# Expert pairs in one block of TensorE, a gather of four experts in two float32r parts, seventeen weight slots

## The chip, the cores and the metric

One core of a Trainium2 chip runs the whole program. The metric is device time in microseconds (us) of one execution. The engines named here: PE (TensorE, matrix products; PEld is its load of stationary operands, which lies beside the products), DVE (VectorE), ACT (ScalarE), POOL (GpSimd) and SP (SyncE), whose queue issues all the DMAs of this kernel in one order.

## The reference, cut to what matters

Two blocks follow each other for 256 tokens of 1024 numbers: a hybrid block (three kinds of token mixing, then a mixture of experts) and a block of feed-forward layers, gating and attention. All is float32. The change lies in the mixture of experts:

```
for gi in range(N_GROUPS):                      # 4 groups of 8 experts
    hg = silu(einsum('nd,edf->nef', x, wg[gi])) * einsum('nd,edf->nef', x, wu[gi])
    y = y + einsum('nef,efd->nd', hg * gates[:, gi, :, None], wd[gi])
```

Each token has two experts of the 32; `gates` is zero for the others. An expert has two matrices of 1024 x 512 and one of 512 x 1024, 6 MB of float32, so the 32 of them are 192 loads of 1 MB.

## The kernel before

Ahead of the experts a mixing stage runs to about 620 us, with its weights split into two float32r parts each (`mm3`, lines 276 to 278: three products for one). After the experts come four feed-forward layers of the same kind, the first through `ffn(0)`.

The expert stage computes only the tokens that an expert has. `route` finds for each expert the rank of every token in its list; `places(p)` makes a one-hot matrix `oh` of 256 tokens by 64 places for each of the two experts of pair p on DVE, and `gather(p)` multiplies the normed tokens `xn` (named `xnr` in the rows) by it on PE, in float32: 16 products of a 128 x 128 stationary operand with 128 columns, in the trace 32 rows. ACT adds shift and gain and writes `xg`. There are 16 pairs, and a gather stands one pair ahead.

`pair` does the rest. `both` takes two weight slots, one for each expert, and issues for every k two products of 64 stationary columns with 512 columns of weights: expert 0 into rows 0 to 63 of a PSUM tile, expert 1 into rows 64 to 127. Where the two stand next to each other on PE they run side by side, in different columns of the array. A pair has four calls of `both` for the gate and up matrices and two for the down matrix, 48 such products, 96 rows (line 1211; a float32 product has two rows). Between them lie four transposes of the activated product (line 1232), two of `oh` (1239), two small products for the gates (1241), and `spread`, eight float32r products (lines 1262, 1263) that bring the pair's result back to the tokens.

In each pair a list `order` fixes the order of the products of `both` among themselves; where the gather's products and those of `spread` stand between them is left to the scheduler of the framework. After every `both`, `load_slot` puts two loads on SP's queue, into the slots just read. There are 19 slots of 1 MB: `wp`, `wr` (half of what held the hi and lo parts of the activations in the mixing stage; the other half holds `xn`), eight `we`, four `wx`, three `ws` and two `whl`, the last two kinds shared with the weight staging of the layers before and after. A load waits until PE has read the slot's old content, and a matrix product until its load has landed. Each load counts on one of eight semaphores in turn, so that a load also waits for the eighth load before it.

After pair 0, `overflow` reads the longest list and branches on all engines around code for lists over 64, which is not run with these inputs (line 1407). PSUM holds a ring of four `mm` tiles for all of this, and four `bg` tiles for `spread`.

Of the kernel before, what the change touches and what calls it, by code (L numbers as in the profile page):

```python
# [8 lines left out]
F32 = mybir.dt.float32  # L9
F32R = mybir.dt.float32r  # L10
# [9 lines left out]
S = 256  # L20
# [13 lines left out]
WS, WHL, WH2 = 3, 3, 3  # L34
NE_B8, NE_MIX, NSLOT = 8, 4, 19
ADA_EVERY, ADA_FROM = 3, 6
# [145 lines left out]
class Program:  # L182
# [280 lines left out]
    def run(self):  # L463
        tc, nc, d = self.tc, self.nc, self.d
        with ExitStack() as es:
# [36 lines left out]
            eights.close()  # L502
            self.parts()
            self.whx = es.enter_context(tc.tile_pool(name="whx", bufs=1))
# [16 lines left out]
            self.last_norm(g)  # L521

    def parts(self):
        self.hi, self.lo = [self.main.tile([128, KT, S], F32R, name=n, tag="hl", bufs=2) for n in ("hi", "lo")]

# [614 lines left out]
    def experts(self):  # L1140


        nc, tc, d, V = self.nc, self.tc, self.d, self.nc.vector
        km, C, exs = self.km, self.cap_limit, self.exs
        iota = km[:, 192:320]
        self.xn, spare = [self.main.tile([128, 2, 1024], F32, name=n, tag="hl", bufs=2) for n in ("xnr", "wr")]
        with tc.tile_pool(name="exw", bufs=1) as self.exw:
            self.slots.append(spare.rearrange("p a c -> p (a c)"))
            self.slots += [self.b8([128, 2048], name="we") for _ in range(NE_B8)]
            xgs = self.b8([128, 2, KT, 2, CAP], name="xg")  # L1150
# [8 lines left out]
            def places(p):  # L1159

                e2 = slice(2 * p, 2 * p + 2)
                ohs[p] = oh = exs.tile([128, 2, 2, CAP], F32, name="oh", bufs=2)
                V.tensor_tensor(oh, iota[:, None, None, :CAP].to_broadcast([128, 2, 2, CAP]),
                                rank[:, :, e2, None].to_broadcast([128, 2, 2, CAP]), op=OP.is_equal)
                if C < CAP:
                    V.memset(oh[..., C:], 0.0)

            def gather(p):

                oh, xg = ohs[p], xgs[:, p % 2]  # L1170
                for k0 in range(0, KT, 4):
                    ps = self.mms().rearrange("p (k a c) -> p k a c", k=4, a=2)
                    for k in range(k0, k0 + 4):
                        for t in range(2):
                            nc.tensor.matmul(ps[:, k - k0], self.xn[:, t, k * 128:k * 128 + 128], oh[:, t], start=(t == 0), stop=(t == 1))  # L1175
                        gain, shift = self.a2c[:, k:k + 1], self.sh2c[:, k:k + 1]
                        nc.scalar.activation(xg[:, k], ps[:, k - k0], AF.Identity, bias=shift, scale=gain)

            places(0)
            gate, rgs = gates()  # L1180
            gather(0)
            pend = None
            for p in range(NE // 2):

                def ahead():
                    if p + 1 < NE // 2:
                        places(p + 1)
                        gather(p + 1)

                pend = self.pair(p, xgs[:, p % 2], ohs[p], gate, yp, pend, ahead)  # L1190
# [11 lines left out]

    def both(self, outs, xs, ks, w, order):


        ws = [self.slots[(self.nuse + j) % NSLOT] for j in range(2)]
        self.nuse += 2
        for k in ks:
            for ps, c in outs:
                for j in range(2):  # L1210
                    ins = self.nc.tensor.matmul(ps[j * 64:j * 64 + 64], xs(k)[j], w(ws[j], k, c), start=(k == 0), stop=(k == order[1]))  # L1211
                    self.chain(order[0], ins)
        for _ in range(2):
            self.load_slot()

    def pair(self, p, xg, oh, gate, yp, pend, ahead):
        nc, exs, V = self.nc, self.exs, self.nc.vector
        e0, order = 2 * p, []
        ps = []
        for z in range(2):  # L1220
            ps.append(self.mms())
            for u in range(2):
                self.both([(ps[z], 0)], lambda k: [xg[:, k, j] for j in range(2)], range(4 * u, 4 * u + 4),
                          lambda w, k, c: w[:, k % 4 * 512:k % 4 * 512 + 512], (order, KT - 1))
        a = exs.tile([128, 512], F32, name="act")
# [5 lines left out]
        for ft in range(4):  # L1231
            nc.tensor.transpose(pt[:, ft * 128:ft * 128 + 128], a[:, ft * 128:ft * 128 + 128], self.ident)  # L1232
        at = exs.tile([128, 4, 2, CAP], F32, name="actT")
        nc.scalar.copy(at.rearrange("p a b c -> p (a b c)"), pt)

        po = self.mms()
        o2 = [oh[:, t].rearrange("p a c -> p (a c)") for t in range(2)]
        for t in range(2):
            nc.tensor.transpose(po[:, t * 128:t * 128 + 128], o2[t], self.ident)
        for t in range(2):  # L1240
            nc.tensor.matmul(po[:, 256:258], o2[t], gate[:, t, e0:e0 + 2], start=(t == 0), stop=(t == 1))
        ot = self.exw.tile([128, S], F32R, name="ot", bufs=2)
# [6 lines left out]
        for h in range(2):  # L1249
            pd = self.mms()  # L1250
            self.both([(pd, 0)], lambda k: [at[:, k, j] for j in range(2)], range(4),
                      lambda w, k, c: w[:, k * 512:k * 512 + 512], (order, 3))
            nc.scalar.activation(dh[:, h], pd, AF.Copy, scale=gs)
            V.scalar_tensor_tensor(dl[:, h], pd, gs, dh[:, h].bitcast(F32), op0=OP.mult, op1=OP.subtract)
        return p, dh, dl, ot, yp

    def spread(self, p, dh, dl, ot, yp):

        for h in range(2):
            for t in range(2):  # L1260
                o = ot[:, t * 128:t * 128 + 128]
                self.nc.tensor.matmul(yp[t][h], o, dl[:, h], start=(p == 0), stop=False)  # L1262
                self.nc.tensor.matmul(yp[t][h], o, dh[:, h], start=False, stop=(p == NE // 2 - 1))  # L1263

    def route(self, km):
# [7 lines left out]
        def sm(n, name):  # L1273
            return small.tile([128, 2, n], F32, name=name)
# [10 lines left out]
        xT = self.whl([128, 2, KT, 128], F32, True)  # L1285
        ss, rs, lg = sm(2, "ssr"), small.tile([128, 2], F32, name="rsr"), sm(36, "lg")
        for h in range(2):
            self.res(0, h)
# [37 lines left out]
        logits(0)  # L1326
        self.chain(edge[1], nc.scalar.activation(self.xn[:, 0], self.x[:, 0], AF.Copy, scale=rs[:, 0:1]))
        evac(1, 0)
# [4 lines left out]
        self.chain(edge[1], nc.scalar.activation(junk[:, :1], self.ones[:, :1], AF.Exp))  # L1333
        self.chain(edge[1], nc.scalar.activation(self.xn[:, 1], self.x[:, 1], AF.Copy, scale=rs[:, 1:2]))
        self.res = self.rest = self.edge = None
# [21 lines left out]
        sel = small.tile([128, 2, NE], F32R, name="sel")  # L1357
        V.tensor_mul(sel.rearrange("p a (g e) -> p a g e", g=4), og4, ssel[:, :, None, :].to_broadcast([128, 2, 4, 8]))
        pk = self.mms()[:, :2 * NE].rearrange("p (a b) -> p a b", a=2)
# [37 lines left out]
    def overflow(self, topi, rgs, iota):  # L1397
# [9 lines left out]
        with tc.If(n > C):  # L1407
            nc.sync.dma_start(rg.rearrange("e p c -> p e c"), rgs)
            with tc.For_i(0, NE) as e:
                with tc.tile_pool(name="ov", bufs=1) as ov:  # L1410
# [8 lines left out]
                    for c0 in range(C, S, 128):  # L1419
# [15 lines left out]
                        for k in range(KT):  # L1435
                            ps = mm()[:, :128]
                            for t in range(2):
                                nc.tensor.matmul(ps, self.xn[:, t, k * 128:k * 128 + 128], oh[:, t], start=(t == 0), stop=(t == 1))
# [4 lines left out]
                        s, at = [exs.tile([128, 512], F32, name=n) for n in ("act", "actT")]  # L1443
                        nc.scalar.activation(s, pz[0], AF.Silu)
# [383 lines left out]
```

## Time and profile before

| | |
|---|---|
| median of 3 runs | 2152.36 us (2151.04 to 2152.95) |
| profiled execution | 2148.5 us, span 2146.7 us |
| PE busy | 2083.3 us, 97% of the span |
| DVE, ACT busy | 1110.4 us (52%), 866.2 us (40%) |
| DMA | 503.20 MB, mean 234 GB/s |
| expert stage, first gather to last `spread` | 636.9 to 1141.8 us |

PE is busy nearly throughout. The slices of the page show that the DMA engines are half idle before and after the expert stage, at some 200 GB/s, and move about 410 GB/s within it. In the views below a window gives, for each engine, busy time and count of instructions, then the granted clock of PE (1.00 is 2.4 GHz, 0.50 is 1.2 GHz), the busy share of the DMA engines and their rate.

### The profile page before, as it was taken

The numbers are of one execution on the slowest core, as the hardware profiler recorded it, in microseconds if no ns is written. First come the engines' busy times: TensorE is split into PE (matmuls) and PEld (weight loads), VectorE is DVE, ScalarE is ACT, GpSimd is POOL, SyncE is SP. The second block draws the span as 40 slices with busy tenths as digits, with TensorE's granted clock in tenths as the row PEclk, the third lists the DMA queues.
The fourth block names the chain that finished last, engine by engine and source line by source line (L and its number), as shares of the span: only waits on it lengthen the run. The fifth ranks groups of instructions, "written<-read, shape, count | busy, mean of one in ns | idle before, by whom it ended". The sixth has DMA issues, their size and how long they took to land.

```text
span 2146.7 us, 29952 instructions
## 1 busy us (share of the span) xinstructions
PE 2083.3 (97%) x12484; PEld 1634.6 (76%) x12484; DVE 1110.4 (52%) x1602; ACT 866.2 (40%) x1264; POOL 24.7 (1%) x40
## 2 busy tenths in 40 slices
PE   7999999999988999999999999999999999999998
PEld 5889889877873444444447998878999999989997
DVE  5987867756450010001006555756555655686555
ACT  4444234344441222122115444645444544475443
POOL 0000000000000000000000000000000000000000
PEclk9999999999999999999999999999999999999999
DMA  8655445565677999999955555544555555533552
GB/s 331 239 192 206 177 174 182 195 233 196 217 303 321 409 416 411 410 396 411 404 209 206 180 193 197 209 174 145 209 182 191 178 180 194 177 118 138 190 183 98
DMA packets 72126, 503.20 MB, mean 234 GB/s; under 512 B 8218, under 2 KB 10034, under 8 KB 11698
## 3 DMA queue, kind: packets, MB, share of 16 engines
q1 hardware_dynamic: 71986, 501.24, 62.0%
q8 instruction: 99, 1.62, 0.3%
q14 instruction: 41, 0.34, 0.0%
HBM read 500.14 MB, written 1.07 MB: 233 GB/s over the span
## 4 chain that ended last, share of the span: by engine, by line
PE 65%; DVE 2%; ACT 1%; issue 0%; DMA 0%; POOLq 0%; DVEq 0%; POOL 0%; ACTq 0%
PE mm L1211 16%; PE mm L276 10%; PE mm L278 10%; PE mm L277 10%; PE bg L276 5%; PE bg L277 5%; PE bg L278 5%; PE mm L1175 3%; PE bg L1262 1%; PE bg L1263 1%; PE mm L419 1%; DVE act L1227 0%; PE mm L1232 0%; PE mm L1780 0%; PE mm L1743 0%
## 5 line engine op out<-in xcount | busy, mean ns | idle before, releaser
L256 DVE TENSOR_TENSOR whl<-ws,whl 128x1024 fp32r<-128x1024 f32 x228 | 277.7, 1220 | 220.9 <-ACT whl L255 220.1
L255 ACT CAST whl<-ws 128x1024 fp32r<-128x1024 f32 x228 | 238.4, 1048 | 295.3 <-PE mm L278 250.1
L256 DVE TENSOR_TENSOR wlx<-ws,whx 128x1024 fp32r<-128x1024 f32 x165 | 201.0, 1222 | 141.2 <-ACT whx L255 140.7
L255 ACT CAST whx<-ws 128x1024 fp32r<-128x1024 f32 x165 | 172.3, 1049 | 175.6 <-PE mm L278 100.3
L276 PE MATMUL mm<-hi,whl 128*128 128x256 f32 x836 | 235.4, 282 | 1.1 <-DVE whl L256 1.0
L277 PE MATMUL mm<-lo,whl 128*128 128x256 f32 x836 | 233.8, 280 | 0.1
L278 PE MATMUL mm<-hi,whl 128*128 128x256 f32 x836 | 233.3, 279 | 0.0
L256 DVE TENSOR_TENSOR whd<-ws,whd 128x1024 fp32r<-128x1024 f32 x113 | 137.7, 1219 | 112.0 <-ACT whd L255 111.2
L255 ACT CAST whd<-ws 128x1024 fp32r<-128x1024 f32 x113 | 118.2, 1046 | 172.7 <-PE mm L278 127.6
L276 PE MATMUL mm<-hi,wlx 128*128 128x256 f32 x640 | 179.4, 280 | 0.5 <-ACT rrow L1545 0.5
L277 PE MATMUL mm<-lo,whx 128*128 128x256 f32 x640 | 179.3, 280 | 0.0
L278 PE MATMUL mm<-hi,whx 128*128 128x256 f32 x640 | 179.2, 280 | 0.0
L276 PEld LDWEIGHTS mm<-hi,whl 128*128 128x128 f32 x836 | 157.2, 188 | 3.3 <-issue 1.2
L277 PEld LDWEIGHTS mm<-lo,whl 128*128 128x128 f32 x836 | 157.2, 188 | 1.5 <-DVE lo L620 0.7
L278 PEld LDWEIGHTS mm<-hi,whl 128*128 128x128 f32 x836 | 157.2, 188 | 0.2
L1227 DVE TENSOR_TENSOR act<-act,mm 128x512 f32<-128x512 f32 x16 | 11.0, 688 | 273.5 <-PE mm L1211 273.5
L276 PEld LDWEIGHTS mm<-hi,wlx 128*128 128x128 f32 x640 | 121.0, 189 | 1.9 <-ACT rrow L1545 0.8
L277 PEld LDWEIGHTS mm<-lo,whx 128*128 128x128 f32 x640 | 121.0, 189 | 0.7
L278 PEld LDWEIGHTS mm<-hi,whx 128*128 128x128 f32 x640 | 121.1, 189 | 0.0
L277 PE MATMUL mm<-whl,hi 128*128 128x512 f32 (+1 forms) x304 | 118.0, 388 | 0.0
L278 PE MATMUL mm<-whl,hi 128*128 128x512 f32 (+1 forms) x304 | 116.3, 383 | 0.0
L276 PE MATMUL mm<-whl,lo 128*128 128x512 f32 (+1 forms) x304 | 114.8, 391 | 1.2 <-DVE lo L433 1.2
(554 smaller groups left out, 4331.5 us busy)
## 6 DMA issues: line engine op xcount, KB each, us to landing
ws<-in_w_fi SPq DMA_DIRECT2D x88, 1024.0 KB, 4.8
we<-in_w_e SPq DMA_DIRECT2D x80, 1024.0 KB, 8.8
ws<-in_w_fo SPq DMA_DIRECT2D x44, 1024.0 KB, 4.7
ws<-in_w_a SPq DMA_DIRECT2D x40, 1024.0 KB, 4.7
wx<-in_w_e SPq DMA_DIRECT2D x40, 1024.0 KB, 8.6
ws<-in_w_e SPq DMA_DIRECT2D x30, 1024.0 KB, 8.8
ws<-in_w_b SPq DMA_DIRECT2D x26, 1024.0 KB, 4.9
whl<-in_w_e SPq DMA_DIRECT2D x20, 1024.0 KB, 6.9
```

The lines of the kernel that those rows point to most:

```text
L255: w1 = nc.scalar.copy(wh[:, :m], src)
L256: w2 = nc.vector.tensor_sub(wl[:, :m], src, wh[:, :m].bitcast(F32))
L276: first = mm(out, ll, rh, start=start, stop=False)
L277: mm(out, lh, rl, start=False, stop=False)
L278: self.last_mm = mm(out, lh, rh, start=False, stop=stop)
L419: ins = nc.tensor.transpose(pss[k % 2][:, (k // 2) * 128:(k // 2) * 128 + 128], self.x[:, t, k * 128:k * 128 + 128], self.ident)
L1175: nc.tensor.matmul(ps[:, k - k0], self.xn[:, t, k * 128:k * 128 + 128], oh[:, t], start=(t == 0), stop=(t == 1))
L1211: ins = self.nc.tensor.matmul(ps[j * 64:j * 64 + 64], xs(k)[j], w(ws[j], k, c), start=(k == 0), stop=(k == order[1]))
L1227: V.tensor_mul(a, a, ps[1])
L1262: self.nc.tensor.matmul(yp[t][h], o, dl[:, h], start=(p == 0), stop=False)
L1263: self.nc.tensor.matmul(yp[t][h], o, dh[:, h], start=False, stop=(p == NE // 2 - 1))
```

## The change

- The gather takes four experts at a time and float32r. `hi` and `lo` are now two tiles of their own for the whole program. In `route` they hold the normed tokens as `hh` (ACT, which wrote `xn` before) and the remainder `hl` (DVE, two new operations of 128 x 1024). A gather of four experts is, for each of the eight k, four products with 256 columns: the remainder and the main part for each half of the tokens. Half of it (four k, 16 products) is issued in each pair, for the four experts after the current ones; pair 0 also does the second half of the first four between its first and second `both`.
- One list `pe` fixes the whole order of PE in the stage: gather, `both`, transposes, `spread`. The products of `both` of a pair are not broken into any more.
- The `spread` of pair 0 is issued ahead of the branch.
- `wr` and one `we` are gone: 17 slots. `xg` takes two tiles instead of one, and `actT` moves to another pool.

The core of the diff:

```diff
-NE_B8, NE_MIX, NSLOT = 8, 4, 19
+NE_B8, NE_MIX, NSLOT = 7, 4, 17
...
-            self.parts()
+            self.hi, self.lo = [main.tile([128, KT, S], F32R, name=n) for n in ("hi", "lo")]
...
+                e4 = slice(4 * q, 4 * q + 4)
+                ohs[q] = oh = exs.tile([128, 2, 4, CAP], F32R, name="oh", bufs=2)
...
+            def gather(q, ks):
+                oh, xg = ohs[q], xgs[q % 2]
+                parts = [(hz, t) for t in range(2) for hz in (self.hl, self.hh)]
+                for k in ks:
+                    if k % 2 == 0:
+                        both = self.mms().rearrange("p (k a c) -> p k a c", k=2, a=4)
+                    ps = both[:, k % 2]
+                    for i, (hz, t) in enumerate(parts):
+                        self.chain(self.pe, nc.tensor.matmul(ps, hz[:, t, k * 128:k * 128 + 128], oh[:, t], start=(i == 0), stop=(i == 3)))
...
+                    if 4 * q < NE:
+                        if p % 2 == 0:
+                            places(q)
+                        gather(q, ks)
...
                 if p == 0:
+                    self.spread(*pend)
+                    pend, self.pe = None, []
                     self.overflow(topi, rgs, iota)
...
+                if p == 0 and z == 0 and u == 0:
+                    gather(0, range(4, KT))
...
+        self.chain(edge[0], V.scalar_tensor_tensor(hl[:, 0], self.x[:, 0], rs[:, 0:1], hh[:, 0].bitcast(F32), op0=OP.mult, op1=OP.subtract))
...
+        self.no_sync(V.scalar_tensor_tensor(hl[:, 1], self.x[:, 1], rs[:, 1:2], hh[:, 1].bitcast(F32), op0=OP.mult, op1=OP.subtract), found)
```

How PE's order changes in a pair well inside the stage. First before: from the transposes of one pair to the first piece of `spread` of the pair before (`k` is the identity, `we`, `wx`, `ws` weight slots, `whd` the result that `spread` brings back; x13 is thirteen in a row).

```order
L1239 MATMUL mm<-k_75,oh 128x128 x2
L1241 MATMUL mm<-gate,oh 128x2 x2
L1175 MATMUL mm<-oh,xnr 128x128 x4
L1211 MATMUL mm<-we,actT 64x512 x13
L1175 MATMUL mm<-oh,xnr 128x128 x4
L1211 MATMUL mm<-we,actT 64x512 x3
L1211 MATMUL mm<-wx,xg 64x512 x2
L1262 MATMUL bg<-whd,ot 128x512
```

The gather of the next pair (L1175) cuts the run of 16 down products after the thirteenth, between the two experts of one k, and `spread` cuts the next pair's gate products. Now after, from the last gate and up products of a pair to the start of its share of the gather:

```order
L1211 MATMUL mm<-ws,xg 64x512 x9
L1264 MATMUL bg<-whd,ot 128x512 x8
L1235 MATMUL mm<-k_75,act 128x128 x4
L1242 MATMUL mm<-k_75,oh 128x128 x2
L1244 MATMUL mm<-gate,oh 128x2 x2
L1172 MATMUL mm<-oh,lo 128x256
L1172 MATMUL mm<-oh,hi 128x256
```

`spread` has moved in one piece between the products and the transposes, which wait for DVE; behind the two last rows the gather goes on to its sixteen products in one piece, and then the 16 down products follow whole.

SP's queue at the start of the stage, before: the reloads behind pair 0 and the branch (`topi` is the longest list).

```order
L1401 TENSOR_LOAD topi
L1401 ISA x2
L1199 DMA wp<-in_w_e 128x2048
L1199 DMA wr<-in_w_e 128x2048
L1199 DMA we<-in_w_e 128x2048 x8
L1199 DMA wx<-in_w_e 128x2048 x2
L1407 COMPARE_AND_BRANCH
```

After:

```order
L1407 TENSOR_LOAD topi
L1407 ISA x2
L1200 DMA wp<-in_w_e 128x2048
L1200 DMA we<-in_w_e 128x2048 x7
L1200 DMA wx<-in_w_e 128x2048 x4
L1413 COMPARE_AND_BRANCH
```

Twelve reloads stand ahead of the branch on either side; those behind it go round 17 slots instead of 19.

On DVE, in `route` after the change, the second new operation stands between the choice of experts and the ranks:

```order
L1361 TENSOR_TENSOR ssel<-rp,ig 128x16
L1363 TENSOR_TENSOR sel<-og,ssel 128x64
L1364 SCALAR_TENSOR_TENSOR lo<-x,rsr,hi 128x1024
L1388 TENSOR_TENSOR wsel<-wsel,ssel 128x16
L1372 TENSOR_SCALAR rank<-sel 128x64
```

Before, the rows follow one another without the third; `rank` is what `oh` and with it the first gather wait for.

## Rows read from the trace of the kernel before

**Rows 1.** The waits of SP's queue, 600 to 1140 us (us, times, longest).

```profile
SPq L1199 <- PE mm L1211: 372.6, 126, 8.6
```

**Rows 2.** Windows of the expert stage (engines, PE clock, DMA share, GB/s).

```profile
650.00:675.00 25.00, 22.34 (x116) 10.89 (x112) 2.92 (x6) 7.63 (x14) 0.00 (x0) 1.00 1.01 423
656.00:660.00 4.00, 3.11 (x23) 2.06 (x20) 1.30 (x4) 0.83 (x2) 0.00 (x0) 1.00 1.02 430
685.00:690.00 5.00, 5.00 (x27) 1.71 (x23) 0.00 (x0) 0.60 (x1) 0.00 (x0) 1.00 0.72 257
737.00:768.00 31.00, 30.11 (x150) 13.35 (x148) 2.93 (x6) 6.55 (x14) 0.00 (x0) 1.00 1.01 413
```

**Rows 3.** PE from pair to pair, timeline (start, us, line, out<-in, xcount, idle before).

```profile
849.80 0.49 PE L1232 MATMUL mm<-k,act 128*128 128x128 f32 x3
...
850.71 1.14 PE L1175 MATMUL mm<-oh,xnr 128*128 128x128 f32 x8
851.78 4.51 PE L1211 MATMUL mm<-we,actT 128*64 128x512 f32 x18
...
861.23 0.40 PE L1263 MATMUL bg<-whd,ot 128*128 128x512 f32 x1
861.46 0.39 PE L1262 MATMUL bg<-whd,ot 128*128 128x512 f32 x1
...
880.25 0.66 PE L1232 MATMUL mm<-k,act 128*128 128x128 f32 x4 [0.89 <-DVE act L1227]
...
883.31 0.59 PE L1211 MATMUL mm<-ws,actT 128*64 128x512 f32 x1
...
883.74 0.59 PE L1211 MATMUL mm<-ws,actT 128*64 128x512 f32 x1
```

**Rows 4.** PE timeline: float32r products with 256 columns, at 1.2 and 2.4 GHz.

```profile
1148.35 0.41 PE L277 MATMUL mm<-whl,hi 128*128 128x256 f32 x1
1148.57 0.41 PE L278 MATMUL mm<-whl,hi 128*128 128x256 f32 x1
...
1161.39 0.28 PE L277 MATMUL mm<-lo,whx 128*128 128x256 f32 x1
1161.51 0.28 PE L278 MATMUL mm<-hi,whx 128*128 128x256 f32 x1
```

**Rows 5.** ACT's and DVE's groups by line that price the new operations.

```profile
L256 DVE TENSOR_TENSOR wlx<-ws,whx 128x1024 fp32r<-128x1024 f32 x165 | 201.0, 1222 | 141.2 <-ACT whx L255 140.7
L1177 ACT ACTIVATE xg<-mm,ada,a2c 128x128 f32<-128x128 f32 x126 | 55.3, 458 | 61.6 <-PE mm L1175 61.6
```

**Rows 6.** PE timeline around the start of the stage and the branch.

```profile
636.94 2.97 PE L1175 MATMUL mm<-oh,xnr 128*128 128x128 f32 x12 [0.44 <-DVE oh L1163]
...
646.73 10.47 PE L1211 MATMUL mm<-we,xg 128*64 128x512 f32 x48
...
672.18 1.05 PE L1175 MATMUL mm<-oh,xnr 128*128 128x128 f32 x8
679.14 6.31 PE L1211 MATMUL mm<-wx,xg 128*64 128x512 f32 x16 [5.91 <-PEq L1407]
685.27 4.03 PE L1211 MATMUL mm<-ws,xg 128*64 128x512 f32 x17
```

**Rows 7.** SP and PE timelines at the end of the stage.

```profile
1093.98 0.33 SPq L1199 DMA_DIRECT2D wr<-in_w_e  x1
...
1135.38 0.59 PE L1211 MATMUL mm<-wp,actT 128*64 128x512 f32 x1
...
1141.42 0.39 PE L1263 MATMUL bg<-whd,ot 128*128 128x512 f32 x1
```

**Rows 8.** DMA time from issue to landing: expert loads, then early ones (`adaf`).

```profile
DMA to landing us min/median/max: 4.7/8.7/13.6
...
DMA to landing us min/median/max: 13.6/16.0/20.4
```

**Rows 9.** Window of the early loads.

```profile
20.00:40.00 20.00, 20.00 (x114) 11.88 (x113) 13.92 (x40) 8.13 (x20) 0.49 (x2) 1.00 1.02 415
```

More of the change, by code (lines that the diff above doesn't have):

```diff
@@ L502, in run @@
             eights.close()
-            self.parts()
             self.whx = es.enter_context(tc.tile_pool(name="whx", bufs=1))
@@ L1145, in experts @@
         iota = km[:, 192:320]
-        self.xn, spare = [self.main.tile([128, 2, 1024], F32, name=n, tag="hl", bufs=2) for n in ("xnr", "wr")]
         with tc.tile_pool(name="exw", bufs=1) as self.exw:
-            self.slots.append(spare.rearrange("p a c -> p (a c)"))
+            self.pe = []
             self.slots += [self.b8([128, 2048], name="we") for _ in range(NE_B8)]
-            xgs = self.b8([128, 2, KT, 2, CAP], name="xg")
+            xgs = [self.b8([128, KT, 4, CAP], name="xg") for _ in range(2)]
             self.slots += [self.exw.tile([128, 2048], F32, name="wx", bufs=NE_MIX) for _ in range(NE_MIX)]
@@ L1157, in experts, with places @@
             ohs = {}
[L1159 to L1164, printed above, removed]
-                if C < CAP:
[L1166 to L1177, printed above, removed]
+            def places(q):
+                e4 = slice(4 * q, 4 * q + 4)
+                ohs[q] = oh = exs.tile([128, 2, 4, CAP], F32R, name="oh", bufs=2)
+                V.tensor_tensor(oh, iota[:, None, None, :CAP].to_broadcast([128, 2, 4, CAP]),
+                                rank[:, :, e4, None].to_broadcast([128, 2, 4, CAP]), op=OP.is_equal)
+                if C < CAP:
+                    V.memset(oh[..., C:].bitcast(F32), 0.0)
@@ L1179, in experts @@
             places(0)
             gate, rgs = gates()
-            gather(0)
+            gather(0, range(4))
             pend = None
             for p in range(NE // 2):
+                q, ks = p // 2 + 1, range(4 * (p % 2), 4 * (p % 2) + 4)
                 def ahead():
[L1186 to L1190, printed above, removed]
+                    if 4 * q < NE:
+                        if p % 2 == 0:
+                            places(q)
+                        gather(q, ks)
+                pend = self.pair(p, xgs[p // 2 % 2], ohs[p // 2], gate, yp, pend, ahead, gather)
@@ L1201, in load_slot, with both @@
             return ins
-    def both(self, outs, xs, ks, w, order):
+    def both(self, ps, xs, ks, last):
         ws = [self.slots[(self.nuse + j) % NSLOT] for j in range(2)]
@@ L1208, in both, with pair @@
         for k in ks:
[L1209 to L1212, printed above, removed]
+            for j in range(2):
+                o = k % 4 * 512
+                self.chain(self.pe, self.nc.tensor.matmul(ps[j * 64:j * 64 + 64], xs[:, k, j], ws[j][:, o:o + 512],
+                                                          start=(k == 0), stop=(k == last)))
         for _ in range(2):
             self.load_slot()
-    def pair(self, p, xg, oh, gate, yp, pend, ahead):
-        nc, exs, V = self.nc, self.exs, self.nc.vector
-        e0, order = 2 * p, []
+    def pair(self, p, xg, oh, gate, yp, pend, ahead, gather):
+        nc, exs, V, pe = self.nc, self.exs, self.nc.vector, self.pe
+        j0, e0 = 2 * p % 4, 2 * p
         ps = []
@@ L1222, in pair @@
             for u in range(2):
-                self.both([(ps[z], 0)], lambda k: [xg[:, k, j] for j in range(2)], range(4 * u, 4 * u + 4),
-                          lambda w, k, c: w[:, k % 4 * 512:k % 4 * 512 + 512], (order, KT - 1))
+                self.both(ps[z], xg[:, :, j0:j0 + 2], range(4 * u, 4 * u + 4), KT - 1)
+                if p == 0 and z == 0 and u == 0:
+                    gather(0, range(4, KT))
         a = exs.tile([128, 512], F32, name="act")
@@ L1250, in pair @@
             pd = self.mms()
-            self.both([(pd, 0)], lambda k: [at[:, k, j] for j in range(2)], range(4),
-                      lambda w, k, c: w[:, k * 512:k * 512 + 512], (order, 3))
+            self.both(pd, at, range(4), 3)
             nc.scalar.activation(dh[:, h], pd, AF.Copy, scale=gs)
@@ L1260, in spread @@
             for t in range(2):
-                o = ot[:, t * 128:t * 128 + 128]
-                self.nc.tensor.matmul(yp[t][h], o, dl[:, h], start=(p == 0), stop=False)
-                self.nc.tensor.matmul(yp[t][h], o, dh[:, h], start=False, stop=(p == NE // 2 - 1))
+                for i, part in enumerate((dl, dh)):
+                    self.chain(self.pe, self.nc.tensor.matmul(yp[t][h], ot[:, t * 128:t * 128 + 128], part[:, h],
+                                                              start=(p == 0 and i == 0), stop=(p == NE // 2 - 1 and i == 1)))
     def route(self, km):
```

31 lines of the change are left out of this document (18 added, 13 removed).

## The prediction

> **What bounds the kernel now.** I read the slices of the page first: PE is busy nearly everywhere, and only in the expert stage are the DMA engines busy too. So the first question is which of the two holds that stage. The waits of SP's queue answer it: from 600 to 1140 us the loads waited 372.6 us, in 126 waits, for PE to have read a slot [rows 1]. No row has PE waiting for a load, and the last expert load was issued at 1094.0 us, long before PE read it at 1135.4 [rows 7]. PE is the bound, with full slots in front of it. But the margin is thin. A pair takes 880.25 - 849.80 = 30.45 us [rows 3]. Its twelve loads of 1.0486 MB make 12.58 MB, so 413 GB/s, which is what the window of one pair shows [rows 2]. Where loads are queued without a gap the rate is 423 GB/s over 25 us [rows 2], so that twelve take 29.7 us. If the loads come to set the pace, a pair cannot go under that, 0.7 us less than now; the rest of a gain lies in the end of the stage, where PE now works on for 48 us after the last load was issued, through the slots that stood full.
>
> **PE's work in a pair, term by term.**
> - The 48 products of `both`, 96 rows, run side by side: one start to the next of a slot is 883.74 - 883.31 = 0.43 us [rows 3]. 48 of these make 20.6 us. The change leaves them, and none is cut in two.
> - `spread`: 861.46 - 861.23 = 0.23 us each [rows 3], eight are 1.9 us, as before.
> - Transposes, `oh` and gates: 850.71 - 849.80 = 0.9 us for a list with one row missing, 1.1 us whole [rows 3].
> - Gather before: 32 rows; eight take 851.78 - 850.71 = 1.07 us [rows 3], four such groups 4.3 us. After: 16 float32r products with 256 columns a pair. The feed-forward layers have the same form, a 128 x 128 operand and 256 columns, at 1161.51 - 1161.39 = 0.12 us [rows 4], so 1.9 us: 2.4 us less.
> - The wait of 0.89 us for the product on DVE ahead of the transposes [rows 3] now has the 1.9 us of `spread` in front of it and goes.
>
> Before: 20.6 + 1.9 + 1.1 + 4.3 + 0.9 = 28.8 us, against 30.45 measured; 1.7 us are the cuts and seams. After: 20.6 + 1.9 + 1.1 + 1.9 = 25.5 us, with seams between 0.2 and 1.7 us: 25.7 to 27.2. ACT has four evacuations of 256 columns to do for the gather of a pair; 128 columns take 458 ns [rows 5], so they take between 1.8 and 3.7 us, and the next reader is the next gate product 7 us later. They are hidden.
>
> **So the DMA becomes the bound.** 25.7 to 27.2 us of PE stand against 29.7 us of loads. With the slots full at first, PE runs ahead, empties them, and from then on waits in front of `both` for about 2.5 to 4 us a pair. The time of the stage is therefore made of the start of the stream of loads, its length, and what PE does after the last.
>
> *Start.* Two new operations of 128 x 1024 on DVE, 1.22 us each by the splits of the same size [rows 5]. The first delays half of the logits (some 0.4 us, an estimate); the second stands whole ahead of the ranks, and `oh` has twice the columns (0.3 us more, an estimate): together 1.9 us, first gather at 638.9 instead of 636.94 [rows 6]. PE is at 1.2 GHz there, where 256 columns take 1148.57 - 1148.35 = 0.22 us [rows 4]: 3.5 us for 16, then 8 x 0.43 = 3.4 us for the first `both`: first slots free at 645.8, against 646.7 [rows 6]. The rest of pair 0: second half of the gather 1.9, three `both` 10.3, the wait of 0.9 (no `spread` is there to cover it), 1.1, gather 1.9, down products 6.9, then ACT and DVE on the result, half of it behind the first four products of `spread`, 6.4 - 3.4 = 3.0 as at the end of the stage [rows 7]: 671.8. Before, the last product ahead of the branch ends at 672.18 + 1.05 = 673.2 [rows 6]. The branch costs 5.9 us of fetch as before, and the first `both` behind it runs at the low clock, 685.27 - 679.14 = 6.1 us [rows 6]: slots free at 683.8 instead of 685.3. After that release the window 685 to 690 us moved 257 of 423 GB/s, so the stream began 1.7 us later [rows 2]; now at 685.5. The twelve reloads ahead of the branch are done by then on either side.
>
> *Length.* 192 loads less 17 before the stage and 12 behind pair 0 leave 163 (before, 161). The two slots fewer thus cost two loads of 2.48 us in the stream, which counts now that it is the bound: 5.0 us. 163 x 1.0486 MB / 423 GB/s = 404.1 us, to 1089.6. While PE frees slots faster than they fill, the stream has no gap: four `both` free eight slots in 14 us, and the 5 us without a release find four loads still waiting.
>
> *End.* From the start of the last `both` to the last `spread` the stage now takes 1141.42 + 0.39 - 1135.38 = 6.4 us [rows 7]; with 0.5 us for the landing, 1096.5. Before: 1141.8. The gain is 45.3 us. The feed-forward loads stand next in SP's queue and land in the 7 us meanwhile; their slots were read four calls of `both` earlier.
>
> The profiled execution took 2148.5 us, 3.9 us under the median of the three runs. Less 45.3 us it would be 2103.2; from the median, **2107 us**, 2.1% faster.
>
> **Unknown costs.** The rate of the stream is read at 423 GB/s with the very loads, which land after 8.7 us, so that three or four are in flight [rows 8]. The early loads landed after up to 20.4 us [rows 8], with some eight in flight, as many as the eight semaphores allow, and ran at 415 [rows 9]; the best short window has 430 [rows 2]. 415 adds 7.8 us, 430 takes 6.6 away. I keep 423, which is the nearest in kind. The delays of the start may be off by 2 us either way.
>
> **Rivals.**
> *PE stays the bound.* Pair 1 starts at 677.7, and PE meets the last load in time as long as a pair takes under (1090.1 + 3.4 - 677.7 - 2.7) / 15 = 27.5 us (2.7 are lost at the low clock behind the branch). Each microsecond above costs 15 us: 28.5 gives 2122, and at 30 us the gain is 8 us. For it: one fixed list makes every wait in it everybody's wait. Against it: between each producer and its reader stands other work, the gather ahead of the down products, `spread` ahead of the transposes.
> *The clock falls while PE waits for loads.* The gap of 5.9 us at the branch lowered the clock: the first `both` behind it took 6.1 us instead of 3.4 [rows 6]. A window with 3.1 us busy in 4 kept 1.00 [rows 2]. With two loads 5.0 us apart and 3.4 us of work each, PE is busy for 69% in part of a pair, between the two. A stretch at 1.2 GHz costs up to 5 us, of which the waits give back 3 to 4; over the seven or so last pairs at most 10 us, 2117. The Trainium skill, page "TensorE: Matmul & The Clock Gate", section "HAM oscillation — how this bites in real kernels", describes such a kernel, which waits for loads in each tile and starts each one at the low clock; that no PE row here waits for a load leaves it open.
> *The stream is slower when the queue is always full.* Slower than before if it falls under 170.9 MB / (1141.8 - 6.9 - 685.5) us = 380 GB/s: eight loads in flight throughout, where now there are three or four. At 360 it would run 475 us, 71 more than above: 2178. Against it: 415 GB/s with eight in flight [rows 9]. The Trainium skill, page "DMA: Bandwidth & Descriptors", section "Bandwidth", says that for transfers between HBM and SBUF the HBM side binds at about 358 GB/s; by that, the time would be some 2180 us. The trace disagrees, with 413 GB/s over a pair [rows 2].
> *The change does not bring the order that it states.* The scheduler's result is known, and PE's order shows the block; 2% for a pair's time unchanged, 2150.
>
> **Numbers.** DMA bound as worked out, 2099 to 2116: 70%. The clock in the waits, to 2120: 9%. PE in part the bound, 2115 to 2146: 12%. Pair time hardly changed or the order without effect, within 0.2% (4.3 us, about what a measurement of this kernel can tell from no change): 4%. The stream slower, over 2157: 5%. So faster 91%, same 4%, slower 5%; the range 2099 to 2124 holds the first two and a part of the third.
>
> **What the profile after would show.** The DMA share at 1.00 and 415 to 425 GB/s from 686 to about 1090 us without the dips; PE rows of line 1211 that wait for loads in the second half of the stage; 16 gather products in one piece at about 0.12 us; the last load issued, eight loads of 2.48 us ahead of its landing, some 27 us before the end of the stage instead of 48. Wrong would be: no waits for loads and a pair of 28 us or more, a granted clock under 1.00 in the middle of the stage, or a rate under 410 with a full queue.

## The result and the profile after

The changed kernel takes 2118.03 us (median of 4 runs, 2116.03 to 2118.75) against 2151.7 us for the kernel before beside it: a ratio of 0.9847, 95% interval 0.9829 to 0.9864, so 33.7 us less. Forecast were 45.3 us and 2107 us, with a range of 2099 to 2124. The measured time lies in the range, but 2 us above the band of the main forecast (DMA bound as worked out, 2099 to 2116). The profiled execution took 2117.9 us, its span is 2116.1 us.

The bound has passed from PE to the loads, as forecast. Windows of the changed kernel (us, busy time of PE, PEld, DVE, ACT, POOL, granted PE clock, DMA share, GB/s):

```profile
689.00:693.00 4.00, 4.00 (x14) 1.31 (x14) 0.00 (x0) 0.00 (x0) 0.00 (x0) 0.65 0.03 10
693.00:697.00 4.00, 4.00 (x22) 1.40 (x19) 0.00 (x0) 0.00 (x0) 0.00 (x0) 1.00 0.45 164
...
700.00:900.00 200.00, 188.91 (x933) 81.70 (x930) 20.97 (x40) 34.94 (x63) 0.00 (x0) 1.00 1.01 420
900.00:1100.00 200.00, 184.22 (x885) 79.45 (x883) 18.21 (x36) 32.88 (x59) 0.00 (x0) 1.00 1.01 421
1100.00:1107.00 7.00, 6.88 (x37) 3.93 (x38) 1.00 (x3) 0.96 (x2) 0.00 (x0) 1.00 1.01 422
```

One window of a pair had 413 GB/s before [rows 2]; now 421 hold for 400 us. The waits of SP's queue, 640 to 1130 us (us, times, longest), answer to [rows 1]:

```profile
SPq L1200 <- PE mm L1211: 125.7, 46, 11.0
SPq L1200 <- DMA we<-in_w_e: 100.3, 50, 3.6
```

SP waits for PE a third as long as before, and twice as long in all (242.8 us over the five kinds of slots) for earlier loads. The page's group of loads says the same: issue to landing takes 19.8 us in place of 8.7 [rows 8], eight loads of 2.49 us:

```profile
we<-in_w_e SPq DMA_DIRECT2D x81, 1024.0 KB, 19.8
```

How long a pair takes is best read from one DVE row of each pair, the product of its two halves. Timeline of DVE in the changed kernel:

```profile
953.41 0.69 DVE L1230 TENSOR_TENSOR act<-act,mm 128x512 f32<-128x512 f32 x1 [12.27 <-PE mm L1211]
981.16 0.69 DVE L1230 TENSOR_TENSOR act<-act,mm 128x512 f32<-128x512 f32 x1 [12.27 <-PE mm L1211]
1010.98 0.69 DVE L1230 TENSOR_TENSOR act<-act,mm 128x512 f32<-128x512 f32 x1 [14.32 <-PE mm L1211]
...
1100.43 0.69 DVE L1230 TENSOR_TENSOR act<-act,mm 128x512 f32<-128x512 f32 x1 [18.11 <-PE mm L1211]
```

From 731 to 981 us a pair takes 27.75 us (one 28.02), PE's own time; the last four take 29.82, which is twelve loads of 2.49 us. PE starts with full slots, gains 2.1 us a pair on the loads, and has used up the lead at about 985 us. Before, by the same row, a pair took 30.6 us at first and 31.4 from 880 us on but for one, 31.0 on average; the forecast's 30.45 us is a little short, since its first row, three transposes, begins behind the first of the four (849.64, so 30.6).

Two places on PE show what was not forecast: the start of the stage, and the gather of half a group (here the one at the end of pair 0, ahead of its down products). The last row stands behind the branch (PE's timeline):

```profile
641.71 0.55 PE L1172 MATMUL mm<-oh,lo 128*128 128x256 f32 x1 [1.41 <-DVE oh L1158]
...
643.56 0.58 PE L1172 MATMUL mm<-oh,lo 128*128 128x256 f32 x1 [0.66 <-ACT xg L1174]
...
646.29 0.58 PE L1172 MATMUL mm<-oh,lo 128*128 128x256 f32 x1 [0.66 <-ACT xg L1174]
...
647.44 1.12 PE L1211 MATMUL mm<-wp,xg 128*64 128x512 f32 x1
...
669.10 0.36 PE L1172 MATMUL mm<-oh,lo 128*128 128x256 f32 x1
...
670.58 0.39 PE L1172 MATMUL mm<-oh,lo 128*128 128x256 f32 x1 [0.77 <-ACT xg L1174]
...
672.44 0.39 PE L1172 MATMUL mm<-oh,lo 128*128 128x256 f32 x1 [0.66 <-ACT xg L1174]
...
673.11 2.37 PE L1211 MATMUL mm<-wx,actT 128*64 128x512 f32 x10
...
688.77 5.53 PE L1211 MATMUL mm<-ws,xg 128*64 128x512 f32 x17 [5.77 <-PEq L1413]
```

Sixteen products take 673.11 - 669.10 = 4.0 us, where 1.9 were forecast. Each PSUM tile takes two indices k side by side. The second one's products wait until ACT has read the first one's half: the rows have 0.77 and 0.66 us of idle time for it, and the starts of the products lie 1.05 and 0.93 us apart there in place of 0.12. The loads of SP's queue around it (start, from the first issue to the last):

```profile
652.77 0.33 SPq L1200 DMA_DIRECT2D wp<-in_w_e  x1
...
693.90 3.76 SPq L1200 DMA_DIRECT2D ws<-in_w_e  x3
...
1079.30 7.79 SPq L1200 DMA_DIRECT2D we<-in_w_e  x4
1089.57 24.34 SPq L219 DMA_DIRECT2D ws<-in_w_fi  x4
```

The first reload goes out at 652.8 us (forecast 645.8), the first behind the branch at 693.9 (forecast 683.8), the last of the stage at 1086.8. PE's end of the stage answers to [rows 7]:

```profile
1086.74 3.65 PE L1211 MATMUL mm<-ws,xg 128*64 128x512 f32 x16 [1.32 <-DMA ws<-in_w_e]
...
1096.68 0.64 PE L1211 MATMUL mm<-wp,xg 128*64 128x512 f32 x1 [1.31 <-DMA wp<-in_w_e]
...
1103.48 7.09 PE L1211 MATMUL mm<-we,actT 128*64 128x512 f32 x32
...
1112.21 1.20 PE L1264 MATMUL bg<-whd,ot 128*128 128x512 f32 x4 [0.51 <-DVE whd L1256]
```

In the gate and up products PE waits 1.3 us every 4.97 us, two loads. The stage ends at 1113.4 us, before at 1141.8.

### The profile page after: what moved, and what is told of

Its sections match the earlier page's. It is cut to its first block, busy times and chain, and to the rows that moved or that the text cites. A ratio compares the mean times of both kernels' runs of the same rounds, so it can differ in the third digit from the quotient of the medians.

```text
span 2116.1 us, 29342 instructions
## 1 busy us (share of the span) xinstructions
PE 2033.4 (96%) x12228; PEld 1611.2 (76%) x12228; DVE 1111.7 (53%) x1596; ACT 846.8 (40%) x1200; POOL 25.0 (1%) x40
## 4 chain that ended last, share of the span: by engine, by line
PE 58%; DMA 6%; ACT 1%; DVE 1%; issue 0%; POOLq 0%; DVEq 0%; POOL 0%; ACTq 0%; SPq 0%
PE mm L1211 11%; PE mm L276 10%; PE mm L278 10%; PE mm L277 10%; PE bg L276 5%; PE bg L277 5%; PE bg L278 5%; DMA wx<-in_w_e 3%; DMA we<-in_w_e 2%; PE bg L1264 1%; DMA wp<-in_w_e 1%; PE mm L1172 1%; ACT xg L1174 1%; PE mm L419 1%; PE mm L1789 0%
## 6 DMA issues: line engine op xcount, KB each, us to landing
we<-in_w_e SPq DMA_DIRECT2D x81, 1024.0 KB, 19.8
wx<-in_w_e SPq DMA_DIRECT2D x44, 1024.0 KB, 19.8
whl<-in_w_e SPq DMA_DIRECT2D x22, 1024.0 KB, 19.8
```

## Experiments

All are timed beside the kernel before (2150 to 2151 us in these runs). Ratios are to it, with 95% intervals. The mixing stage ends at different times from execution to execution: its last product starts between 625.45 and 628.78 us in the fourteen traces, in kernels built from either side. So where a few us decide, the length of the expert stage in the trace, from the first gather product to the end of the last `spread`, is the safer measure: 471.7 us in the changed kernel (1113.4 - 641.7), 504.9 before.

**1. Is it ACT's read that costs the half gather 2 us?** The changed kernel, where ACT reads a PSUM tile only when the products of both its k are done:

```
-   gain, shift = self.a2c[:, k:k + 1], ...
-   nc.scalar.activation(xg[:, k], ps, ...)
+   for e in (k - 1, k) if k % 2 else ():
+       gain, shift = self.a2c[:, e:e + 1], ...
+       nc.scalar.activation(xg[:, e], both[:, e % 2], ...)
```

> The changed kernel with one edit: in the gather ACT reads a PSUM tile only after the products of both its k, so that PE does not wait 0.66 us for ACT twice in each half gather (4.0 us instead of the forecast 1.9). Theory (the stage is set by the stream of loads at 421 GB/s, and only what delays its start counts): the three half gathers of pair 0 get 2.1 us shorter each, less time is spent at the low clock, the rest is hidden: 2110 to 2113, against 2118. Rival (the waits in the fixed order set the pace of every pair): 16 x 2.1 us less, 2085.

Measured: 2107.65 us, 0.9800 (0.9783 to 0.9816), 10.4 us under the change. PE's and DVE's rows in its trace:

```profile
827.69 0.36 PE L1172 MATMUL mm<-oh,lo 128*128 128x256 f32 x1
...
829.76 4.08 PE L1212 MATMUL mm<-ws,actT 128*64 128x512 f32 x17
```

```profile
824.91 0.69 DVE L1231 TENSOR_TENSOR act<-act,mm 128x512 f32<-128x512 f32 x1 [12.27 <-PE mm L1212]
850.72 0.69 DVE L1231 TENSOR_TENSOR act<-act,mm 128x512 f32<-128x512 f32 x1 [12.27 <-PE mm L1212]
880.54 0.69 DVE L1231 TENSOR_TENSOR act<-act,mm 128x512 f32<-128x512 f32 x1 [16.28 <-PE mm L1212]
```

The half gather takes 2.07 us and a pair 25.8: the forecast's size. From 850 us on a pair takes 29.8, eight pairs before the end instead of four. So the pair's 2 us bought nothing in the stream; the gain is at its start. The first reload comes 8.3 us behind the first gather product (647.59 - 639.25) instead of 11.1, and the load behind the branch at 686.52 instead of 693.90. Of these 7.4 us, 2.5 are an earlier end of the mixing stage in this execution, the other 4.9 the waits. By the trace the stage takes 464.6 us, 7.1 less than in the changed kernel, within the theory's 5 to 8; that the time is 2.4 us under its 2110 is the earlier end of the mixing stage.

**2. Does the hole in the loads at the branch cost its length?** The changed kernel with `if p == 0` ahead of `overflow` made `if p == 8`.

> The changed kernel with the branch around the overflow code moved from behind pair 0 to behind pair 8. Theory (stream of loads): the gap of the stream at the branch, 6 to 7 us without a byte around 689 to 695 us, goes, because at pair 8 up to eight loads are in flight while PE stands, and PE's lost 6 us are taken up by its waits for loads: 2110 to 2113. Rival (PE sets the pace): the branch costs PE the same wherever it stands, 2117 to 2119.

Measured: 2111.85 us, 0.9824 (0.9807 to 0.9840), as the theory had it; of the 6.2 us the stage itself gives 4.6 (467.1 us). Windows of its trace:

```profile
660.00:700.00 40.00, 36.27 (x186) 16.50 (x184) 4.20 (x9) 8.16 (x16) 0.00 (x0) 1.00 0.98 405
900.00:920.00 20.00, 13.54 (x56) 5.21 (x56) 0.75 (x1) 1.28 (x2) 0.00 (x0) 0.83 1.01 417
920.00:940.00 20.00, 17.70 (x94) 7.80 (x92) 3.19 (x6) 4.39 (x8) 0.00 (x0) 1.00 0.82 333
```

The loads run through at 690 us. A shorter hole opens behind the branch's new place, 18% of 20 us.

**3. What is the fixed order worth?** The changed kernel without it: gather, transposes and `spread` are left to the scheduler again (no `self.chain` around them), and only the products of `both` are ordered within a pair.

> The changed kernel without the one fixed order of PE: only the products of a pair's gate, up and down matrices keep their order among themselves, as before the change; gather, transposes and spread stand where the scheduler puts them. Theory (stream of loads, 29.9 us a pair): PE's pair grows from about 27.6 us to at most 29.5 us by the cuts, which stays hidden: 2114 to 2122. Rival (keeping the products in one block is what gained the time): 1.5 us a pair or more come back, 2135 to 2145.

Measured: 2130.05 us, 0.9903 (0.9886 to 0.9919), between the two. PE's waits, 720 to 1110 us:

```profile
PE bg L1265 <- DVE whd L1257: 13.7, 9, 1.6
PE mm L1236 <- DVE act L1231: 10.2, 12, 0.9
```

The two waits that the change covers are back: that of `spread` for its operand, which the next pair's products covered, and that of the transposes for DVE, which `spread` covered. Its pairs take (1107.93 - 698.39) / 14 = 29.25 us on average by the DVE rows, as many as 30.2, though no gather product waits for ACT there. PE is late to the end: SP issues the last expert load at 1078.6 us, PE works until 1122.9. The changed kernel's 14 pairs take (1100.43 - 704.32) / 14 = 28.3 us with the loads as the bound, and above that a pair counts: 14 x 0.95 = 13 us, against 12.0 measured.

**4. Is the float32r gather needed?** The kernel before with the order and what goes with it: one list for PE, the first gather in two halves, `spread` of pair 0 ahead of the branch, and ACT behind the products of a PSUM tile. The gather stays float32 with two experts, and there are nineteen slots.

> The kernel before with the fixed order of PE alone (and the first pair's spread ahead of the branch, the first gather in two halves, ACT reading behind the products of a whole PSUM tile): float32 gather of two experts, 19 slots, no second part of the tokens. Theory (stream of loads): PE's pair is about 28.3 us, under 29.9; two loads fewer in the stream, 5 us, and no extra DVE work at the start, 2 us: 2106 to 2113, faster than the changed kernel. Rival (the float32r gather of four is needed): PE's pair of over 30 us, 2125 or more.

Measured: 2107.85 us, 0.9802 (0.9786 to 0.9818), the same as experiment 1. DVE's rows:

```profile
970.73 0.69 DVE L1233 TENSOR_TENSOR act<-act,mm 128x512 f32<-128x512 f32 x1 [12.27 <-PE mm L1215]
998.20 0.69 DVE L1233 TENSOR_TENSOR act<-act,mm 128x512 f32<-128x512 f32 x1 [12.27 <-PE mm L1215]
1026.11 0.69 DVE L1233 TENSOR_TENSOR act<-act,mm 128x512 f32<-128x512 f32 x1 [12.71 <-PE mm L1215]
1055.93 0.69 DVE L1233 TENSOR_TENSOR act<-act,mm 128x512 f32<-128x512 f32 x1 [14.61 <-PE mm L1215]
```

A pair takes 27.47 us, 3.1 to 4 less than before with the same products, and meets the loads two pairs before the end. This bundle brings more than the whole change, and as much as the change with ACT's read moved (experiment 1): the cheaper gather finds PE no longer in demand. No run takes the parts of the bundle one by one.

**5. Both edits of 1 and 2 together.**

> The changed kernel with both of the single edits: ACT reads a PSUM tile of the gather only when the products of both its indices k are done, and the branch stands behind pair 8. Theory A (once TensorE needs 25.8 us for a pair, the 175 loads behind the first 17 set the end, and what is left to gain is the hole in them at the branch): loads run from 647.6 us at 2.49 us each without a hole, pairs grow to 29.8 us early on, the stage ends near 1093 and the time is 2096 to 2101 us, that is about 8 us below the first edit alone (2107.65). Rival B (the stage is still set by TensorE, so that the place of the branch only moves its 10.7 us): 2106 to 2110 us.

Measured: 2106.45 us, 0.9796 (0.9780 to 0.9813): hardly below experiment 1, so theory A's time was missed. B's time came, but not for its reason: the last pairs take 29.8 us by DVE's rows, so PE isn't the bound. The loads have a hole. DVE's rows, windows, and the rows of the branch's line (engine, operation, count, ns, first and last start):

```profile
1058.31 0.69 DVE L1231 TENSOR_TENSOR act<-act,mm 128x512 f32<-128x512 f32 x1 [16.26 <-PE mm L1212]
1088.13 0.69 DVE L1231 TENSOR_TENSOR act<-act,mm 128x512 f32<-128x512 f32 x1 [18.10 <-PE mm L1212]
```

```profile
916.00:920.00 4.00, 4.00 (x22) 1.42 (x20) 0.75 (x1) 0.69 (x1) 0.00 (x0) 1.00 0.76 315
920.00:924.00 4.00, 4.00 (x22) 1.29 (x18) 0.75 (x1) 0.69 (x1) 0.00 (x0) 1.00 0.13 51
924.00:928.00 4.00, 4.00 (x20) 1.29 (x18) 0.00 (x0) 0.00 (x0) 0.00 (x0) 1.00 0.71 260
```

```profile
L1414 SPq EVENT_SEMAPHORE  x8: 17/17/17, 911.2 to 923.7; - x8
...
L1414 PEldq COMPARE_BRANCH  x1: 5952/5952/5952, 887.9 to 887.9; - x1
...
L1414 SPq COMPARE_BRANCH  x1: 50/50/50, 902.6 to 902.6; - x1
```

PE crosses the branch in 6 us and is back at work at 894. SP, behind in its queue, reaches it at 902.6 and issues its next load at 923.83, 21.3 us after it had issued the last. Between stand eight instructions on semaphores, as many as the semaphores that the loads count on, spread over 12.5 us. That they wait for the eight loads in flight fits (the engines fall idle as the last ends), but no row names what they wait for. With the queue run empty 4.0 x (0.24 + 0.87 + 0.29) = 5.6 us are lost.

**6. The kernel of 4 with the branch behind pair 8.**

> The kernel before with a fixed order of TensorE, float32 gather of two experts and nineteen slots, and with the branch behind pair 8. Theory A: its pair takes 27.47 us of TensorE against 25.8 us with the float32r gather, so that with the hole in the loads gone it is TensorE that ends last: from the first pair at 658.8 us, 15 pairs of 27.47 us and 10.7 us for the branch give 1082 us for the product of the last pair and 1096 us for the stage's end, against 1099.7 us measured with the branch behind pair 0: 2103 to 2105 us, 4 to 8 us above the float32r kernel with the same two edits. Rival B (the loads set both, and two more slots are worth 5 us): 2092 to 2097 us, below the float32r kernel.

Measured: 2100.57 us, 0.9768 (0.9752 to 0.9784), the best whole kernel of this study, 17.5 us below the change. It is between the theories in time. Its pairs take 27.47 us but for the one with the branch (38.75) and the last (29.31): PE sets nearly all of it, as A has it, but it comes out 5.9 us below the float32r kernel of 5, not above. The hole at the branch is the same (900 to 940 us: DMA share 0.90 here, 0.87 there).

**7. Are the two slots the difference between 5 and 6?** `NE_B8, NSLOT = 8, 19` made `6, 17` in 6.

> The float32 kernel of f32_branch with seventeen slots of weights in place of nineteen, so that its slots are those of evac_branch. Theory A (evac_branch stays 5.9 us behind f32_branch because it has two slots less: two more loads of 2.49 us behind the start, and two less in reserve at the branch): 2104 to 2108 us, within 2 us of evac_branch (2106.45), with the last pairs at 29.8 us. Rival B (it is the float32r gather itself, for instance its reads by ACT or its start): it stays at 2100 to 2102 us.

Measured: 2108.51 us (2104.24 to 2108.69), 0.9798 (0.9780 to 0.9816), the place of 5 again, half a microsecond past A's range. The stage takes 462.2 us, against 457.5 in 6 and 461.9 in 5: 4.8 us for two loads. With seventeen slots the float32 gather is as fast as the float32r one, whose room takes the other two.

**8. The same from the other side.** `NE_B8, NSLOT = 7, 17` made `5, 15` in the changed kernel.

> The changed kernel with fifteen slots of weights in place of seventeen. Theory A: its last four pairs take 29.8 us each because the loads set them, so that two more loads behind the start cost 2 x 2.49 = 5 us: 2121 to 2125 us, and the pairs grow from 27.75 to 29.8 us two or three pairs earlier. Rival B (the longer pairs at the end are TensorE's own, for instance its clock or its order): no change, 2116 to 2120 us.

Measured: 2121.20 us, 0.9872 (0.9855 to 0.9888), 3.2 us above the change by the medians. The stage takes 476.9 us, 5.2 more than in the changed kernel, so that two loads fewer ahead cost two loads here as well. Pairs turn from 27.75 to 29.8 us a pair or two earlier, as A says. DVE's rows:

```profile
924.26 0.69 DVE L1230 TENSOR_TENSOR act<-act,mm 128x512 f32<-128x512 f32 x1 [12.27 <-PE mm L1211]
952.68 0.69 DVE L1230 TENSOR_TENSOR act<-act,mm 128x512 f32<-128x512 f32 x1 [12.95 <-PE mm L1211]
982.63 0.69 DVE L1230 TENSOR_TENSOR act<-act,mm 128x512 f32<-128x512 f32 x1 [14.44 <-PE mm L1211]
```

**9. Are the loads what stretches the last pairs?** In the changed kernel all loads after the first seventeen move `[:, :1024]` of their slot alone.

> The changed kernel whose loads, but for the first seventeen, move only the first half of the columns of each weight tile, so that half of that traffic is left out and the values are not those of the reference. Theory A: without the loads as a bound every pair takes TensorE's own 27.75 us to the end, the last four too (29.8 us in the changed kernel); the last pair comes 8 us earlier and the time is 2107 to 2111 us. Rival B (the longer pairs at the end have another cause than the loads): they stay at 29.8 us, 2116 to 2119 us. Rival C (the stream of loads also slows the pairs of 27.75 us): all pairs get shorter than 27 us.

Measured: 2099.79 us (one run). DVE's rows of its last pairs:

```profile
1031.64 0.69 DVE L1231 TENSOR_TENSOR act<-act,mm 128x512 f32<-128x512 f32 x1 [12.27 <-PE mm L1212]
1059.37 0.69 DVE L1231 TENSOR_TENSOR act<-act,mm 128x512 f32<-128x512 f32 x1 [12.27 <-PE mm L1212]
1084.11 0.68 DVE L1231 TENSOR_TENSOR act<-act,mm 128x512 f32<-128x512 f32 x1
```

At 27.73 us to the end, so the loads it was; and not below 27.7 at half the traffic, so the stream doesn't slow PE (rival C falls). The last pair takes 24.74 us since no gather follows pair 14, which the expectation forgot. The time fell by more than it said for that reason (3 us), and because the mixing stage ended 2.6 us earlier and pair 0 with the branch took 2.5 us less.

**10 and 11. What the branch costs.** The kernels of 5 and 6 without `overflow`.

> evac_branch with the overflow branch left out (the path for an expert with more tokens than its places is missing; it isn't taken with these inputs). Theory A (crossing the branch empties SyncE's queue of loads, a hole of 5.2 us in a stream that sets the end): the loads run without a hole, 2100 to 2102 us, all pairs from the seventh or eighth on at 29.8 us. Rival B (the hole is made up from loads that were ahead, or its cause is another): 2104 us or more.

> f32_branch with the overflow branch left out (as in evac_nobr). Theory A: TensorE gets back the 11.3 us that the pair with the branch is longer, but the loads, which end 4 us earlier without the hole, take over as the bound: 2095 to 2098 us, with the last four to six pairs at 29.8 us in place of 27.47. Rival B (TensorE alone sets the end): 11 us less, 2088 to 2091 us.

Measured: 2101.92 us, 0.9776 (0.9759 to 0.9792), and 2098.08 us, 0.9760 (0.9744 to 0.9776). In 10 the loads run at 421 GB/s from 660 to 1080 us without a hole, and the 4.5 us (5.9 by the stages, 456.0 against 461.9) are the hole of 5:

```profile
660.00:1080.00 420.00, 394.20 (x1918) 168.30 (x1918) 40.99 (x80) 71.17 (x131) 0.00 (x0) 1.00 1.01 421
```

In 11 PE gets 11.3 us back and the kernel 2.5, since the last three pairs turn to 29.8 us and more: the loads are the floor there too.

**12. The branch where no loads are left to issue.** In 6, behind pair 14.

> f32_branch with the branch behind pair 14, where all loads of expert weights have been issued. Theory A: the stream has no hole, but TensorE pays the whole branch close to the end with nothing behind it to make it up, and SyncE crosses it only when the loads in flight have landed, so that the feed-forward's first loads are issued some 10 us later: 2100 to 2108 us, not better than f32_branch (2100.57). Rival B (the 4 us hole is what f32_branch still loses): 2096 to 2099 us.

Measured: 2105.31 us (2104.02 to 2109.41), 0.9796 (0.9778 to 0.9814), 4.7 us worse than behind pair 8. The pair with the branch is the last and takes 37.96 us by DVE's rows, with nothing behind it to make it up; the first feed-forward load is issued at 1085.8 us instead of 1078.1, 21.9 us behind the last expert load instead of 8.6. Theory A holds.

## Why the prediction was right, and where it was off

- **The bound changes from PE to the loads:** right. Share and rate, the waits of PE for loads late in the stage, and the last load 26.6 us before the end (27 forecast) are as written; experiments 8 and 9 show that the slots and the loads decide. The rate was forecast at 423 GB/s and is 421: 1.9 us.
- **PE's work in a pair, 25.7 to 27.2 us:** wrong by the 1.9 us for the gather after the change and by "They are hidden" for ACT's evacuations. The forecast asked when `xg` is read next, not when PE writes the other half of the same tile. The half gather took 4.0 us and the pair 27.75; without the wait 2.07 and 25.8 (experiment 1). The Trainium skill, page "Perfetto Trace Analysis", section "Optimizing Tensor Performance", asks for independent groups of products to go to different PSUM banks, so that the reading of one lies beside the next; the 0.66 to 0.77 us here are what it costs where two groups share a tile. In the stream it cost nothing, since the loads need 29.8. The forecast's limit for PE, 27.5 us a pair, was too low: by the rows the last fourteen pairs take 28.3 us on average with the loads as the bound, and PE, at 27.75 us a pair, has caught up with the loads four pairs before the end.
- **Start, 685.5 us:** this is where it was lost. Behind the mixing stage's last product the first gather stood 13.0 us (641.71 - 628.71) against 11.5 before, so the 1.9 us for DVE were 1.5. But gather and first `both` took 11.1 us to the reload, not 6.9. Two gaps of 0.66 us lie in the gather, and PE stayed at 1.2 GHz until about 650.5 us (granted clock 0.50 from 641.0 to 650.5), which the forecast had for the gather only. With the waits in the two half gathers that follow ahead of the branch, the stream began to flow near 695.4 us (the window up to 697 us moved 164 GB/s over 4 us, which is 1.6 us at 421): 9.9 us late, of which 3.3 came from the mixing stage.
- **These 3.3 us are not the change's.** The program there is the same; the clock was lower in some spells, as from 520 to 540 us. The same spell at 0.91 and a mixing stage as late, its last product at 628.78 us, stand in the trace of experiment 7, which is built from the kernel before. Before and after:

```profile
520.00:540.00 20.00, 18.05 (x93) 14.56 (x92) 12.19 (x16) 8.19 (x13) 0.00 (x0) 1.00 0.43 162
```

```profile
520.00:540.00 20.00, 18.05 (x88) 14.78 (x87) 13.91 (x18) 8.29 (x12) 0.00 (x0) 0.91 0.53 202
```

- **Length, 404.1 us:** some 411 by the rows. 1.9 us are the rate. The rest, 5.2 us, is a term that was not there: with 19.8 us from issue to landing, the feed-forward loads issued from 1089.57 us move beside the last expert loads. From 695.4 to 1106.6 us (1086.8 + 19.8) 421 GB/s make 173.1 MB, and the 163 loads are 170.9; the 2.2 MB between are 5.2 us. The forecast counted them as if the queue served one after the other. A second count from the trace gives a little less: behind 1106.6 us the DMA engines still move 200 GB/s for 7.3 us, 1.5 MB, of the three feed-forward loads issued by 1094.6 us, so that 1.7 of their 3.1 MB went before, 4 us of the stream. That feed-forward bytes moved ahead of the last expert load is thus shown by the windows; that the time falls by as much without them is not tested.
- **End, 6.4 us and 0.5 for the landing:** right as a sum (1113.4 - 1106.6 = 6.8). But PE didn't wait for the last loads: it waited for a load last at 1096.68 and was at work for the 16.7 us behind it but for 0.5, to read the last slot at about 1107.0 (16 of the 32 rows from 1103.48 on), half a microsecond behind the landing. Both paths end together here.
- **The sum:** 1096.5 forecast, 1113.4 measured. Mixing stage 3.3, start 6.6, rate 1.9, shared engines 5.2, end -0.1: 16.9 us. Behind the stage the program took 2.2 us less than before, so the profiled execution missed the 2103.2 us forecast for it by 14.7. From the median the miss is 11.0, since the forecast had added 3.9 us for a profiled execution before that was faster than its median; these stand against the 3.3 of the mixing stage.
- **Two slots fewer are two loads, 5.0 us:** right. The medians of experiments 7 and 8 put 8 and 3 us on two slots; by the stages, which leave the mixing stage out, it is 4.8 and 5.2.
- **The range:** it holds 2118 only because it was widened to 2124 for the clock in the waits and for PE as part of the bound. Neither came as told: the clock stayed at 1.00, and PE at 27.75 us a pair ran ahead of the loads until 985 us. The mechanism is the one with the 70%; that the time came into the range with the start 6.6 us and the length 7.1 us off, and only 2.2 us of it made up behind the stage, is in part luck.
- **Rivals:** the clock did not fall where PE waited for loads: 1.00 from 900 to 1100 us, with 1.3 us idle in 5. The Trainium skill, page "TensorE: Matmul & The Clock Gate", section "HAM oscillation — how this bites in real kernels", has a kernel whose waits for loads are longer than the work between them start each tile at the low clock; the waits here are shorter than the work, and don't show it. The start of the stage, a gather with two gaps of 0.66 us behind an idle stretch, stayed at 0.50 for 9.5 us. Nor did the stream slow with a full queue: 421 GB/s over 400 us. The Trainium skill, page "DMA: Bandwidth & Descriptors", section "Bandwidth", gives 425 GB/s for 16 MB on one core whose neighbour is idle (issued by GpSimd, here SP issues), and about 358 where both stream; the forecast cited the second figure, and the measurement agrees with the first.
- **What was not forecast at all:** the two halves of the change do not add up. The new gather without the order gains 20 us (experiment 3). The order with the float32 gather, nineteen slots and ACT's read moved gains 42 (experiment 4), and so does the changed kernel with ACT's read moved (experiment 1). Once the order stands, the float32r gather relieves an engine that is no longer the bound, and pays with two slots of the one that is.

## What to carry to other kernels

When a change moves the bound from an engine to the loads, time the stage by when the stream starts, how many loads it has, and what interrupts it; relief of the engine beyond that is worth nothing, and buffers given up for it cost a load each (4.8 and 5.2 us for two slots here). When a PSUM tile is filled in parts, look when its reader starts: the next part's write may wait for that, whatever the reader's result is needed for. Put a branch where the queue that issues loads is least missed, and count its crossing for each engine separately.

## What the runs showed of the hardware

- One core's loads of 1 MB, eight in flight, ran at 421 GB/s for 420 us without a break (experiment 10), whether PE was at its own pace or waited.
- Crossing the branch over code that is not run left PE idle for 5.8 to 5.9 us, with a granted clock of 0.65 in the 4 us behind it (the changed kernel); SP, in whose queue eight loads were in flight, issued no load for some 21 us (experiment 5).
- Matrix products that write one half of a PSUM tile waited until ACT had read the other: mostly 0.66 to 0.77 us of idle time each, 22.8 us over 32 waits in the stage (the changed kernel). The profile puts the waits down to ACT's read; with the read behind both halves they are gone (experiment 1).
